# Row norms and final sums of the last projection listed behind the bank copy, three pairs of row tiles, another product order in the last pair, first-weight sums listed later, staging loads issued by GpSimd

## The chip, the core and the metric

The kernel runs on one core of a Trainium2 chip. The metric is the device time of one execution in microseconds (us), the median of several executions. All arithmetic is float32 or float32 split into two rounded parts.

## What is computed

One encoder layer is applied to two sequences of 1024 rows by 1024 channels (called 0 and 1 here). Cut to what matters:

```python
xn = rmsnorm(x, g_pre)
fv, fg, hv, hg, mg = split(xn @ w_in)
y_f = (real(fft2(fv)) * silu(fg)) @ w_fourier_out
v, x1, x2 = split(short_conv(hv))
z = v
for n, gate in enumerate((x1, x2)):
    z = gate * long_conv(z, filter[n])
y_h = (z * silu(hg)) @ w_hyena_out
g_f, g_h = split(sigmoid(mg + b_merge))
out = (g_f * y_f + g_h * y_h) @ w_out
return x + rmsnorm(out, g_post)
```

The last two lines are where most of the change lies: the last projection with `w_out`, then for each row of 1024 numbers the mean of the squares, its inverse root, the product with `g_post` and the sum with `x`.

## The kernel before

Every float32 operand of TensorE is split into a rounded part h and a rest l, and a product is three matmuls, h·h, h·l and l·h (`mm3`, `times`). ScalarE rounds (a CAST to h), and VectorE or GpSimd subtracts (the l). In rows of the profile, `wh` and `wl` are these parts of a weight block, `bh` and `bl` those of a data block.

There are three stages.

- `phase_fourier` makes the Fourier branch.
- `phase_main` first makes the filters' spectra, with projections of sequence 0 in between (`spill_gate`, `inproj`). In this stretch GpSimd subtracts the `wl` of each half weight block (128 by 512), one in 5 to 10 us, and TensorE waits in order for each of them. It then runs `branches`: the short and the long convolutions, first of sequence 0, then of sequence 1. For sequence 0 the weight parts are made and kept in DRAM (`d_w`); for sequence 1 they are loaded again by SyncE's queue (L728). The same queue loads the filter spectra (`k<-d_k`, L799) and stores results. During sequence 1 the generator `staging` (L912 ff.) reads blocks of three operands of the coming stage from DRAM in 24 pieces of 128 by 1024 (tiles `draw`, in two rooms, one for each half), GpSimd folds each piece in place (four subtractions or additions of 128 by 256), and GpSimd's queue stores it to `d_t` (and, unfolded, `d_wo` for `w_out`). The loads were issued by SyncE (L926), and the scheduler places them behind the load of a filter spectrum. Queues and engines work in order, so a load that waits for its room holds up whatever SyncE has listed behind it.
- `phase_blocks` does the rest of the projections as 34 jobs. A job makes a 256 by 1024 result from a 256 by 1024 and a 1024 by 1024 operand with seven block products instead of eight. Each product is 12 matmuls of 128 columns of weights and 512 columns of data, so a job is 84 matmuls. The products accumulate in three banks of PSUM, PA, PB and PC.

In `phase_blocks` the order on each engine is written by hand: every step is put in a list with a time, `at(t, step)`, the list is sorted, and each engine runs its own steps in this order. A job starts every 7 units, T = 7i. Job i's seven products stand at T + 0 ("11"), 2 ("12"), 3 ("s2"), 4 ("s3"), 6 ("s1"), and, within job i+1's first half, 8 ("s4") and 12 ("22"). So the order on TensorE within a job is: 11, s4 of the job before, 12, s2, s3, 22 of the job before, s1. The step that this text calls the bank copy is `seed` (L1142): ScalarE copies PA, which holds product 11, into PB, and only then may product 12 add to PB. Product s4 of the job before is the cover for that copy. `keep` (L1150) copies PA twice more, to `us` (U) and `m` (V), and `result` combines the banks with these copies into the four quarters (j, n) of a job's result: j is one of two blocks of rows or channels, n a half of 512 columns.

The last eight jobs (26 to 33, kind "o") are the last projection. Each makes two blocks of 128 rows. For each quarter `row_half` has ScalarE square it and sum the squares (`sq`, L1364, into `ss`), and VectorE multiply it with `g_post` (`o<-o,gp` or `o<-pg,gp`). `finish` then does the rest of the row norm on VectorE: an addition, two scalings and three Newton steps of three operations (L1375, L241 to L252; the case of one row has ten operations, L244 to L247), and four operations of 128 by 512 that multiply a quarter with the inverse root and add `x` (L177, `o<-o,rs,xr`), each followed by a store to the output from SyncE. `finish` of job i stood at T + 14, which is time 0 of job i+2. It is listed there ahead of quarter (1,1) of job i+1 (`o<-pg,m`), of that quarter's square on ScalarE, and of the bank copy of job i+2, which stands behind the square. The rows' tiles `o` took turns in two pairs of rooms (`xh4` to `xh7`), and `x` was loaded into one pair (`xh0`, `xh1`; `fetch_row`).

The weights of a job are prepared in `weights`: two blocks cast as they are ("11", "12"), then four sums on VectorE (`sum1`, `sum2`), and the casts and rests of the sums (`s2`, `s13`, `s4`) and of block "22". For the first job all of this stood some 24 units ahead of time 0, so ahead of the first bank copy at time 1.

Of the kernel before, what the change touches and what calls it, by code (L numbers as in the profile page):

```python
# [9 lines left out]
F32 = mybir.dt.float32  # L10
# [6 lines left out]
P = 128  # L17
D = 1024
# [143 lines left out]
class K:  # L162
# [748 lines left out]
    def staging(self):  # L911

        nc, a = self.nc, self.a
        before = None
        for q, k, half in [(q, k, h) for q in (1, 2, 5) for k in range(4) for h in range(2)] + [(0, 0, 0)]:
            r = None
            if q:
                s = slice(256 * half, 256 * half + 256)
                if half:
                    r = self.stage2.tile([P, 4, 256], F32, tag="draw2", name="draw", bufs=1)  # L920
                else:
                    r = self.cp.tile([P, 4, 256], F32, tag="draw", name="draw", bufs=1)
                with self.tc.issue_after(self.spectrum.ins):
                    for i in range(2):
                        src = {1: self.d_g[0][0], 2: self.d_sh[0]}[q][k + 4 * i] if q < 5 else a["w_out"][(k + 4 * i) * P:(k + 4 * i + 1) * P]
                        nc.sync.dma_start(r[:, 2 * i:2 * i + 2], src.rearrange("p (n c) -> p n c", n=2)[:, :, s])  # L926
            if before:
                q_, k_, s_, r_ = before
                if q_ == 5:
                    nc.gpsimd.dma_start(self.d_wo[:, k_, :, s_], r_)  # L930
                self.fold("pool", [r_[:, j] for j in range(4)])
                nc.gpsimd.dma_start(self.d_t[q_][:, k_, :, s_], r_)
            before = q, k, s, r
            yield
# [68 lines left out]
    def phase_blocks(self):  # L1003
# [24 lines left out]
        with ExitStack() as es:  # L1028
# [24 lines left out]
            def weights(j, t11, t12, ts, ts2, ts13, ts4, t22):  # L1053

                def part(t, n, pool, tags, bufs, src):

                    def open_():
                        A[j, n] = [pool.tile([P, 4, P], F32R, tag=g, name=g, bufs=bufs) for g in tags]
                    at(t, open_)
                    halve(t, lambda: (f2(A[j, n][0]), f2(A[j, n][1]), src()))  # L1060
                part(t11, "11", wp, ("wh", "wl"), 2, lambda: raw[j][:, 0])
                part(t12, "12", wp, ("wh", "wl"), 2, lambda: raw[j][:, 1])

                def sum1():
# [194 lines left out]
            for k in range(4):  # L1259
                at(start + 1 + 3 * k, xraw, k)  # L1260
                at(start + 3 + 3 * k, xfold, k)
            weights(0, start + 14, start + 14.1, start + 14.6, start + 15.8, start + 16, start + 16.2, start + 16.4)
            at(start + 11, load_raw, 1)

            PLACES = (None, ("X0", "X1", "E", "G1", "G2", "G0", "X2"), ("X3", "G3", "X0", "X1", "E", "G1", "G2"),
# [11 lines left out]
            for i in range(N):  # L1277
                T = SLOTS * i
                if i == N - 8:
                    at(T - 0.5, self.open_rows, op, jobs, gw)  # L1280
                kind = jobs[i][0]
                last = i + 1 == N
                for n, t in ((0, 0), (1, 2), (2, 3), (3, 4), (4, 6)):
                    at(T + t, product, i, n)
                if not last:
                    at(T + 8, product, i, 5)
                    at(T + 12, product, i, 6)
                at(T + 1, seed, i)
                at(T + 4, keep, i, U)
# [4 lines left out]
                result(i, 0, 0, T + 3.05)  # L1294
                result(i, 1, 1, T + 7.3)
                if not last:
                    result(i, 0, 1, T + 9.05)
                    result(i, 1, 0, T + 13.05)
# [4 lines left out]
                    weights(i + 1, T + 3.2, T + 4.3, T + 4.9, T + 5.7, T + 7.4, T + 9.3, T + 13.2)  # L1303
                    q = operand[i + 1]
                    if q != operand[i]:
                        turn(i, q)
                else:
                    def end():
                        pd = PC[i, 1] = self.psum("mm", 4, "pg")
                        self.times(pd, A[i, "22"], B[5, 3], True)  # L1310
                    at(T + 7, end)
                    at(T + 7.6, lambda: self.tt("dve", U[i], PC[i], U[i], SUB))

                    def row1():
                        self.tt("dve", self.rows[i][2][1][:, 0:512], PC[i, 1], U[i], ADD)
# [17 lines left out]

    def open_rows(self, op, jobs, gw):
        nc, a = self.nc, self.a
        self.op, self.jobs = op, jobs
        self.rows = {}
        self.gp = []
        for n in range(2):
            self.gp.append(gw.tile([P, 512], F32, tag="f", name="gp", bufs=4))  # L1340
            nc.sync.dma_start(self.gp[n], a["g_post"][0][512 * n:512 * n + 512].partition_broadcast(P))

    def open_row(self, i):
        xp = self.xp
        _, u, t = self.jobs[i]
        b, half = u // 2, u % 2
        row = [512 * half + P * t[j] for j in range(2)]
        ss = self.op.tile([P, 2, 2], F32, tag="ss", name="ss", bufs=2)
        o = [xp.tile([P, D], F32, tag=f"xh{4 + 2 * (i % 2) + j}", name="o", bufs=1) for j in range(2)]
        self.rows[i] = [b, row, o, None, ss]  # L1350

    def fetch_row(self, i):
        b, row = self.rows[i][:2]
        x = self.rows[i][3] = [self.xp.tile([P, D], F32, tag=f"xh{j}", name="xr", bufs=1) for j in range(2)]
        for j in range(2):
            self.nc.sync.dma_start(x[j], self.a[f"x{b}"][row[j]:row[j] + P, :])

    def row_half(self, at, t, i, j, n, src, made):
        nc = self.nc
# [9 lines left out]
    def finish(self, i, *rows):  # L1369
        nc, a, op = self.nc, self.a, self.op  # L1370
        b, row, o, x, ss = self.rows[i]
# [3 lines left out]
        nc.vector.tensor_tensor(s1, ss[:, rows[0]:rows[-1] + 1, 0], ss[:, rows[0]:rows[-1] + 1, 1], op=ADD)  # L1375
        self.rstd(op, rs, s1, n)
        for q, j in enumerate(rows):
            for n in (1, 0):
                s = slice(512 * n, 512 * n + 512)
                self.stt("dve", o[j][:, s], o[j][:, s], rs[:, q:q + 1], x[j][:, s], MUL, ADD)  # L1380
                nc.sync.dma_start(a[f"y{b}"][row[j]:row[j] + P, s], o[j][:, s])


def _chan_order():
    o = []
# [72 lines left out]
```

## Time and profile before

| what | us |
|---|---|
| median of three executions (2452.84 to 2453.99) | 2453.25 |
| profiled execution | 2460.39 |
| its span, from the first to the last instruction | 2458.49 |
| TensorE busy within the span | 2370.1 |
| VectorE busy | 2037.7 |
| ScalarE busy | 1126.2 |
| GpSimd busy | 561.7 |

The profile is of one execution, in us from its first instruction. Its own time is 1.90 above its span and 7.14 above the median. PE is TensorE's matmuls and PEld its weight loads, DVE is VectorE, ACT ScalarE, POOL GpSimd and SP SyncE; a q behind a name means the engine's queue, where DMAs are issued. In a row of the timeline stand the start, the duration, the engine, the line, the operation with the tiles that it writes and reads, the shape, and in brackets the idle time before it and what ended that. A row with a count merges neighbours that are alike. The duration of a matmul (0.39) is longer than the distance to the next one, since matmuls overlap. The granted clock is the share of TensorE's full clock.

### The profile page before, as it was taken

What the parts mean: (1) busy time and instruction counts of PE and PEld (TensorE: products, weight loads), DVE (VectorE), ACT (ScalarE), POOL (GpSimd) and SP (SyncE); (2) the same over time, 40 slices, a digit from 0 to 9 for tenths busy, and PEclk for the clock granted to TensorE, in tenths of its full rate; (3) what the DMA queues carried; (4) which work ended last, traced back from release to release, by engine and by line L of the source; (5) the groups of instructions that cost most, each with busy time, mean ns of one, the idle gap of its engine ahead of it and who ended that gap; (6) DMA issues with size and microseconds to landing.
All of it is one profiled execution on the core that took longest, in us unless ns stands there. A gap on an engine that the chain in (4) does not pass through costs nothing. (4 is left out here: it accounts for less than half of the span.)

```text
span 2458.5 us, 37126 instructions
## 1 busy us (share of the span) xinstructions
PE 2370.1 (96%) x13006; PEld 2055.8 (84%) x13006; DVE 2037.7 (83%) x3816; ACT 1126.2 (46%) x2088; POOL 561.7 (23%) x520
## 2 busy tenths in 40 slices
PE   6999999999989999999999999999999999999997
PEld 6988888888878988888889888888788888888775
DVE  7686788888889999999899999986667687776876
ACT  5545666666654333334222223233334466665532
POOL 1341222212234333442032333412100000101000
PEclk9999999999999999999999999999999999999999
DMA  8535644454556455555465667643556679888544
GB/s 272 173 136 196 221 157 157 156 160 161 166 190 202 161 178 176 160 161 195 151 212 184 215 206 228 214 141 112 205 180 219 234 260 286 257 275 244 160 153 137
DMA packets 253762, 470.26 MB, mean 191 GB/s; under 512 B 24502, under 2 KB 100503, under 8 KB 253192
## 3 DMA queue, kind: packets, MB, share of 16 engines
q1 hardware_dynamic: 230828, 393.12, 49.3%
q0 software_dynamic: 22560, 74.77, 9.2%
q8 instruction: 102, 1.67, 0.3%
q14 instruction: 84, 0.69, 0.1%
q10 hardware_dynamic: 188, 0.02, 0.0%
HBM read 300.04 MB, written 167.77 MB: 190 GB/s over the span
## 5 line engine op out<-in xcount | busy, mean ns | idle before, releaser
L194 PE MATMUL pin<-xh,wh 128*128 128x512 f32 x1472 | 578.1, 394 | 9.8 <-DMA wh<-d_w 5.6
L194 PE MATMUL pin<-xh,wl 128*128 128x512 f32 x1472 | 576.8, 393 | 4.2 <-DMA wl<-d_w 3.2
L194 PE MATMUL pin<-xl,wh 128*128 128x512 f32 x1472 | 577.9, 393 | 0.0
L181 POOL TENSOR_TENSOR wl<-wr,wh 128x512 fp32r<-128x512 f32 x136 | 252.8, 1859 | 748.1 <-ACT wh L171 719.8
L194 PEld LDWEIGHTS pin<-xh,wh 128*128 128x128 f32 x1472 | 278.1, 189 | 61.7 <-DMA wh<-d_w 6.4
L194 PEld LDWEIGHTS pin<-xh,wl 128*128 128x128 f32 x1472 | 278.1, 189 | 56.4 <-DMA wl<-d_w 4.1
L194 PEld LDWEIGHTS pin<-xl,wh 128*128 128x128 f32 x1472 | 278.2, 189 | 50.9
L194 PE MATMUL pT<-cinv,yh 128*128 128x256 f32 x1024 | 192.2, 282 | 0.0
L194 PEld LDWEIGHTS pT<-cinv,yh 128*128 128x128 f32 x1024 | 164.6, 190 | 9.4 <-ACT yh L171 0.4
L181 POOL TENSOR_TENSOR draw<-draw 128x256 f32<-128x256 f32 x96 | 108.9, 1134 | 250.2 <-DMA draw<-d_g 143.5
L181 DVE TENSOR_TENSOR t<-pX,k 128x1024 f32<-128x1024 f32 x128 | 155.5, 1215 | 8.3 <-PE pX L194 7.3
L171 ACT CAST yh<-y 128x512 fp32r<-128x512 f32 x128 | 79.5, 621 | 177.9 <-DVE y L181 152.0
L194 PE MATMUL pX<-bh,cfwd 128*128 128x256 f32 x768 | 160.5, 287 | 0.0
L171 ACT CAST wh<-wr 128x512 fp32r<-128x512 f32 x136 | 83.8, 616 | 159.3 <-PE pin L194 110.2
L171 ACT CAST bh<-b 128x512 fp32r<-128x512 f32 x144 | 88.7, 619 | 131.3 <-DVE b L181 90.7
L194 PE MATMUL pT<-cinv,yl 128*128 128x256 f32 x512 | 144.9, 283 | 1.1 <-DVE yl L181 1.1
L194 PEld LDWEIGHTS pX<-bh,cfwd 128*128 128x128 f32 x768 | 125.7, 191 | 3.1
L181 DVE TENSOR_TENSOR bl<-b,bh 128x512 fp32r<-128x512 f32 x144 | 112.1, 780 | 13.2 <-ACT bh L171 13.2
L194 PE MATMUL pX<-bl,cfwd 128*128 128x256 f32 x384 | 109.3, 285 | 0.0
L181 DVE TENSOR_TENSOR yl<-y,yh 128x512 fp32r<-128x512 f32 x128 | 92.7, 725 | 10.7 <-ACT yh L171 10.6
L1231 POOL DMA_DIRECT2D d_m<-gt x32 | 27.5, 860 | 320.7 <-DVE gt L181 290.5
L194 PEld LDWEIGHTS pT<-cinv,yl 128*128 128x128 f32 x512 | 97.7, 191 | 3.5 <-DVE yl L181 1.6
(351 smaller groups left out, 5712.5 us busy)
## 6 DMA issues: line engine op xcount, KB each, us to landing
k<-d_k SPq DMA_DIRECT2D x128, 512.0 KB, 4.4
wr<-in_w_in SPq DMA_DIRECT2D x136, 256.0 KB, 3.2
d_g<-gt SPq DMA_DIRECT2D x92, 256.0 KB, 2.6
d_k<-kt SPq DMA_DIRECT2D x128, 128.0 KB, 2.2
d_k<-kt SPq DMA_DIRECT2D x64, 256.0 KB, 2.3
fz<-d_g SPq DMA_DIRECT2D x64, 256.0 KB, 5.3
d_w<-wh POOLq DMA_DIRECT2D x48, 256.0 KB, 4.0
d_w<-wl POOLq DMA_DIRECT2D x48, 256.0 KB, 4.8
```

What stands on the lines that cost most here:

```text
L171: self.rounded = nc.scalar.copy(h, src)
L181: return e.tensor_tensor(out, a, b, op=op)
L194: return self.nc.tensor.matmul(out, lhsT, rhs, start=start, stop=stop, skip_group_check=shared)
L1231: at(t + 0.3, lambda: nc.gpsimd.dma_start(d_m[:, c], box[0], accum_op=ADD))
```

## The change

There are five edits.

1. `staging`: the loads of the pieces are issued by GpSimd and no longer by SyncE.
2. The first job's sums and all that follows from them are listed at times 0.2 to 2.4, behind the first bank copy.
3. `finish` is split in two. `root` holds the small operations and stands at T + 15.3, which is 1.3 of job i+2. `finish` holds the four long operations and stores, at T + 17.7 (3.7 of job i+2). Both are now behind the bank copy of job i+2 at its time 1.
4. Since rows live longer, `o` takes turns in three pairs of rooms (`xh2` to `xh7`), and `x` of odd jobs goes to rooms of its own (one tile of `op`, two tiles `f`). Each half row of `x` is a load of its own, four per job where there were two, and they stand at T + 5.3 (before: T + 8.9, in the last job T + 3).
5. The last pair: product 22 of job 32 stands at T + 9 (before: T + 12), and the last job's products 12, s2 and s3 stand one unit later. So TensorE's order in the last job is 11, s4 of job 32, 22 of job 32, 12, s2, s3, s1, and the closing two as before. The quarter (1,0) and the norm of job 32 move forward with it, ahead of quarter (1,1) of job 33. In the last job the inverse root of block 0 now stands ahead of the sums of block 1.

```diff
@@ staging
-  nc.sync.dma_start(r[:, 2 * i:2 * i + 2], src.rearrange("p (n c) -> p n c", n=2)[:, :, s])
+  nc.gpsimd.dma_start(r[:, 2 * i:2 * i + 2], src.rearrange("p (n c) -> p n c", n=2)[:, :, s])
@@ phase_blocks
-  weights(0, start + 14, start + 14.1, start + 14.6, start + 15.8, start + 16, start + 16.2, start + 16.4)
+  weights(0, start + 14, start + 14.1, 0.2, 1.1, 1.3, 2.1, 2.4)
...
+  early = i == N - 2
-  for n, t in ((0, 0), (1, 2), (2, 3), (3, 4), (4, 6)):
+  for n, t in enumerate((0, 3, 4, 5, 6) if last else (0, 2, 3, 4, 6)):
...
-  at(T + 12, product, i, 6)
+  at(T + (9 if early else 12), product, i, 6)
...
-  at(T + (8.9 if not last else 3), self.fetch_row, i)
+  at(T + 5.3, self.fetch_row, i)
...
-  at(T + 14, self.finish, i, 0, 1)
+  rows = [0, 1]
+  at(T + (11.3 if early else 15.3), self.root, i, rows)
+  at(T + (12.6 if early else 17.7), self.finish, i, rows)
...
-  at(T + 8.9, self.finish, i, 1)
+  at(T + 8.5, self.root, i, [1])
...
-  at(T + 10, self.finish, i, 0)
+  at(T + 9.4, self.root, i, [0])
+  at(T + 9.5, self.finish, i, [1])
+  at(T + 10, self.finish, i, [0])
@@ open_row, fetch_row
-  o = [xp.tile([P, D], F32, tag=f"xh{4 + 2 * (i % 2) + j}", name="o", bufs=1) for j in range(2)]
+  o = [xp.tile([P, D], F32, tag=f"xh{2 + 2 * (i % 3) + j}", name="o", bufs=1) for j in range(2)]
...
-  x = self.rows[i][3] = [self.xp.tile([P, D], F32, tag=f"xh{j}", name="xr", bufs=1) for j in range(2)]
+  if i % 2:
+      f = self.op.tile([P, D], F32, tag="xr", name="xr", bufs=1)
+      x = [[f[:, 0:512], f[:, 512:1024]], [self.gw.tile([P, 512], F32, tag="f", name="xr", bufs=4) for _ in range(2)]]
+  else:
+      x = [self.xp.tile([P, D], F32, tag=f"xh{j}", name="xr", bufs=1) for j in range(2)]
+      x = [[t[:, 0:512], t[:, 512:1024]] for t in x]
```

What this does to the order of instructions is seen at three places. The first is VectorE in a job in the middle of the last projection. Before, from the end of the norm of job i-2 on (the last Newton step, `rs`) to the rests `wl` of the next weights:

```order
L252 SCALAR_TENSOR_TENSOR rs<-rs_t,rs 128x2
L177 SCALAR_TENSOR_TENSOR o<-o,rs,xr 128x512 x4
L181 TENSOR_TENSOR o<-pg,m 128x512
L181 TENSOR_TENSOR o<-o,gp 128x512
L181 TENSOR_TENSOR s13l<-wraw,s13h 128x1024
L181 TENSOR_TENSOR o<-pg,gp 128x512
L181 TENSOR_TENSOR s4l<-wraw,s4h 128x512
L181 TENSOR_TENSOR o<-pg,gp 128x512
L181 TENSOR_TENSOR wl<-wraw,wh 128x512 x2
```

After, the same stretch (the eleven operations of `root` between L1387 and `o<-pg,gp` are left out):

```order
L181 TENSOR_TENSOR o<-pg,m 128x512
L181 TENSOR_TENSOR o<-o,gp 128x512
L181 TENSOR_TENSOR s13l<-wraw,s13h 128x1024
L1387 TENSOR_TENSOR s_25130<-ss 128x2
...
L181 TENSOR_TENSOR o<-pg,gp 128x512
L181 TENSOR_TENSOR s4l<-wraw,s4h 128x512
L181 TENSOR_TENSOR o<-pg,gp 128x512
L181 TENSOR_TENSOR wl<-wraw,wh 128x512
L177 SCALAR_TENSOR_TENSOR o<-o,rs,xr 128x512 x4
L181 TENSOR_TENSOR wl<-wraw,wh 128x512
```

The quarter `o<-pg,m`, for whose square the bank copy stands in line, has no norm ahead of it any more; the twelve small and the four long operations come later in the same job.

The second place is ScalarE at the first job. Before, the casts of the sums stand ahead of the bank copy (`pg<-pg`):

```order
L1034 CAST wh<-wraw 128x512
L768 COPY gt<-pin_19513 128x512
L1034 CAST s2h<-wsum 128x512
L1034 CAST s13h<-wraw 128x1024
L1034 CAST s4h<-wraw 128x512
L1034 CAST a2h<-wraw 128x512
L1142 COPY pg<-pg 128x512
```

After:

```order
L1034 CAST wh<-wraw 128x512
L768 COPY gt<-pin_19513 128x512
L1142 COPY pg<-pg 128x512
L1034 CAST s2h<-wsum 128x512
L1034 CAST s13h<-wraw 128x1024
L1034 CAST s4h<-wraw 128x512
L1034 CAST a2h<-wraw 128x512
```

Four casts have gone from ahead of the copy to behind it.

The third place is GpSimd in the stretch of the filters' spectra, far ahead of where the pieces were folded before. Before, from the load of the inverse tables (`cinv`) on, there stand only subtractions of weight rests, up to the first store of a kept weight block:

```order
L899 DMA cinv<-in_c_inv 128x6144
L181 TENSOR_TENSOR wl<-wr,wh 128x512 x53
L735 DMA d_w_0_0_189<-wh 128x512
```

After, from the twenty-eighth of them on (`d_g_0_4` and `d_g_0_1`, `d_g_0_5` are results that the same stretch stores to DRAM):

```order
L181 TENSOR_TENSOR wl<-wr,wh 128x512 x28
L926 DMA draw<-d_g_0_4_129 128x2x256 x2
L181 TENSOR_TENSOR wl<-wr,wh 128x512
L181 TENSOR_TENSOR draw<-draw 128x256 x8
L932 DMA d_t_241<-draw 128x4x256
L181 TENSOR_TENSOR wl<-wr,wh 128x512
L932 DMA d_t_241<-draw 128x4x256
L926 DMA draw<-d_g_0_1_126 128x2x256 x2
L181 TENSOR_TENSOR wl<-wr,wh 128x512 x6
L926 DMA draw<-d_g_0_5_130 128x2x256 x2
L181 TENSOR_TENSOR wl<-wr,wh 128x512
L181 TENSOR_TENSOR draw<-draw 128x256 x8
```

The folds of the first operand, two pieces at a time, now stand between subtractions that TensorE waits for; there are four such pairs in this stretch and at the start of `branches`. Those of the second operand follow as its blocks are stored, the first pair in the last part of sequence 0 and the others in sequence 1. On SyncE the 48 loads are gone. The order of the convolutions of sequence 1 on TensorE, VectorE and ScalarE, which the scheduler sets, differs in places as well.

More of the change, by code (lines that the diff above doesn't have):

```diff
@@ L1286, in phase_blocks @@
                     at(T + 8, product, i, 5)
-                    at(T + 12, product, i, 6)
+                    at(T + (9 if early else 12), product, i, 6)
                 at(T + 1, seed, i)
-                at(T + 4, keep, i, U)
+                at(T + (5 if last else 4), keep, i, U)
                 at(T + 7, keep, i, V)
@@ L1292, in phase_blocks @@
                     at(T + 2.9, self.open_row, i)
-                    at(T + (8.9 if not last else 3), self.fetch_row, i)
-                result(i, 0, 0, T + 3.05)
+                    at(T + 5.3, self.fetch_row, i)
+                result(i, 0, 0, T + (4.05 if last else 3.05))
                 result(i, 1, 1, T + 7.3)
@@ L1297, in phase_blocks @@
                     result(i, 0, 1, T + 9.05)
-                    result(i, 1, 0, T + 13.05)
+                    result(i, 1, 0, T + (10.05 if early else 13.05))
                     if kind == "o":
-                        at(T + 14, self.finish, i, 0, 1)
+                        rows = [0, 1]
+                        at(T + (11.3 if early else 15.3), self.root, i, rows)
+                        at(T + (12.6 if early else 17.7), self.finish, i, rows)
                     if i + 2 < N:
                         at(T + 6.7, load_raw, i + 2)
-                    weights(i + 1, T + 3.2, T + 4.3, T + 4.9, T + 5.7, T + 7.4, T + 9.3, T + 13.2)
+                    weights(i + 1, T + 3.2, T + 4.3, T + 4.9, T + 5.7, T + 7.4, T + 9.3, T + (10.3 if early else 13.2))
                     q = operand[i + 1]
@@ L1335, in open_rows @@
         nc, a = self.nc, self.a
-        self.op, self.jobs = op, jobs
+        self.op, self.jobs, self.gw = op, jobs, gw
         self.rows = {}
@@ L1348, in open_row @@
         ss = self.op.tile([P, 2, 2], F32, tag="ss", name="ss", bufs=2)
-        o = [xp.tile([P, D], F32, tag=f"xh{4 + 2 * (i % 2) + j}", name="o", bufs=1) for j in range(2)]
-        self.rows[i] = [b, row, o, None, ss]
+        o = [xp.tile([P, D], F32, tag=f"xh{2 + 2 * (i % 3) + j}", name="o", bufs=1) for j in range(2)]
+        self.rows[i] = [b, row, o, None, ss, {}]
     def fetch_row(self, i):
         b, row = self.rows[i][:2]
-        x = self.rows[i][3] = [self.xp.tile([P, D], F32, tag=f"xh{j}", name="xr", bufs=1) for j in range(2)]
+        if i % 2:
[4 more added lines that the diff above has]
+            x = [[t[:, 0:512], t[:, 512:1024]] for t in x]
+        self.rows[i][3] = x
         for j in range(2):
-            self.nc.sync.dma_start(x[j], self.a[f"x{b}"][row[j]:row[j] + P, :])
+            for n in range(2):
+                self.nc.sync.dma_start(x[j][n], self.a[f"x{b}"][row[j]:row[j] + P, 512 * n:512 * n + 512])
     def row_half(self, at, t, i, j, n, src, made):
@@ L1367, in row_half, with root @@
         at(t + d + 0.05, lambda: self.mul("dve", self.rows[i][2][j][:, s], src(), self.gp[n]))
-    def finish(self, i, *rows):
-        nc, a, op = self.nc, self.a, self.op
-        b, row, o, x, ss = self.rows[i]
+    def root(self, i, rows):
+        nc, op = self.nc, self.op
+        ss, rs_ = self.rows[i][4:6]
         n = len(rows)
@@ L1377, in finish @@
         for q, j in enumerate(rows):
+            rs_[j] = rs[:, q:q + 1]
+    def finish(self, i, rows):
+        nc, a = self.nc, self.a
+        b, row, o, x, _, rs = self.rows[i]
+        for j in rows:
             for n in (1, 0):
                 s = slice(512 * n, 512 * n + 512)
-                self.stt("dve", o[j][:, s], o[j][:, s], rs[:, q:q + 1], x[j][:, s], MUL, ADD)
+                self.stt("dve", o[j][:, s], o[j][:, s], rs[j], x[j][n], MUL, ADD)
                 nc.sync.dma_start(a[f"y{b}"][row[j]:row[j] + P, s], o[j][:, s])
```

## The prediction

> **What bounds the kernel now.** I read the page first, then the waits of TensorE over the whole span.
>
> ```profile
> span 2458.5 us, 37126 instructions
> PE 2370.1 (96%) x13006; PEld 2055.8 (84%) x13006; DVE 2037.7 (83%) x3816; ACT 1126.2 (46%) x2088; POOL 561.7 (23%) x520
> ...
> PE pg L194 <- ACT pg L1142: 14.3, 9, 2.9
> ...
> PE pin L194 <- DMA wh<-d_w: 5.6, 3, 4.5
> ...
> PE pin L194 <- DMA wl<-d_w: 3.2, 2, 3.1
> ```
>
> TensorE bounds the kernel: it stands idle for 88 us of 2458.5. No edit takes matmuls away, so every gain must come from this idle time, or from a slow clock behind it. A row of the waits gives the sum, the number of waits and the longest. The largest that the change touches is that for the bank copy: 14.3 us in 9 waits. Those for weights loaded by SyncE are 8.8 us in 5.
>
> A matmul costs (1777.43 - 1774.71) / 12 = 0.2267 us by these starts, so a product of 12 takes 2.72 and a job of 84 takes 19.04.
>
> ```profile
> 1774.71 0.39 PE L194 MATMUL pg<-xh,wh 128*128 128x512 f32 x1
> ...
> 1777.43 0.39 PE L194 MATMUL pg<-xh,wh 128*128 128x512 f32 x1
> ...
> 1780.66 0.79 PE L194 MATMUL pg<-xh,wh 128*128 128x512 f32 x1 [2.85 <-ACT pg L1142]
> ```
>
> **Part 1, the norm behind the bank copy.** The chain of waits names product 12 of jobs 27 and 33; the timeline shows what stands ahead of the second.
>
> ```profile
> 2298.66 11.19 PE pg L194 x48
> ...
> 2424.48 11.19 PE pg L194 x48
> ```
>
> ```profile
> 2417.49 0.15 DVE L1375 TENSOR_TENSOR s<-ss 128x2 f32<-128x2 f32 x1
> ...
> 2419.85 2.74 DVE L177 SCALAR_TENSOR_TENSOR o<-o,rs,xr 128x512 f32<-128x512 f32 x4
> 2422.51 0.68 DVE L181 TENSOR_TENSOR o<-pg,m 128x512 f32<-128x512 f32 x1
> ```
>
> ```profile
> 2417.46 0.59 ACT L1150 COPY m<-pg 128x512 f32<-128x512 f32 x1 [1.21 <-PE pg L194]
> 2423.22 0.63 ACT L1364 ACTIVATE sq<-o 128x512 f32<-128x512 f32 x1 [4.23 <-DVE o L181]
> ...
> 2423.85 0.58 ACT L1142 COPY pg<-pg 128x512 f32<-128x512 f32 x1
> ```
>
> `m` is ready at 2418.05, but `o<-pg,m` starts at 2422.51, because VectorE has begun the norm at 2417.49. The square and the bank copy follow, and product 12 starts at 2424.48, when the copy ends. From 2298.66 to there are six jobs: 125.82 us where six times 19.04 are 114.2. The excess is 11.6.
>
> With the norm behind it, `o<-pg,m` can start when `m` is there. Counted from the start S of product 11: `m` S + 0.6, the quarter S + 1.3, its square S + 1.9; product 11 ends at S + 2.9, the copy at S + 3.5. Product s4 covers TensorE until S + 5.44, so the copy has 1.9 us to spare and the stall goes whole. What is late next is VectorE's other work.
>
> ```profile
> 2403.53:2424.48 20.95, 19.33 (x84) 15.68 (x84) 15.29 (x33) 8.13 (x18) 0.00 (x0) 1.00 0.37 119
> ```
>
> In this row of the table of windows (length; then busy time of PE, PEld, DVE, ACT, POOL; granted clock), VectorE is busy for 15.29 of 20.95, and would be for 15.29 of 19.04. A hand-made schedule leaves about 1.3 us at the tightest wait. I take **-11.6**, with -5.8 as the poor end (half the stalls return) and nothing beyond.
>
> The three pairs of rooms and the separate `x` rooms only keep rows longer. The `x` loads (four issues where there were two) stand behind the stores and ahead of the next raw weights on SyncE, which then waits for a room; SyncE has the time of a job for some twelve issues, so I cost them at nothing. If that cover were gone, the raw weights would come late.
>
> **Part 2, the end.**
>
> ```profile
> 2440.81 2.74 DVE L177 SCALAR_TENSOR_TENSOR o<-o,rs,xr 128x512 f32<-128x512 f32 x4
> 2443.46 0.68 DVE L181 TENSOR_TENSOR o<-pg,m 128x512 f32<-128x512 f32 x1
> 2447.69 0.15 DVE L1375 TENSOR_TENSOR s<-ss 128x1 f32<-128x1 f32 x1
> 2449.79 1.42 DVE L177 SCALAR_TENSOR_TENSOR o<-o,rs,xr 128x512 f32<-128x512 f32 x2
> ...
> 2453.81 1.42 DVE L177 SCALAR_TENSOR_TENSOR o<-o,rs,xr 128x512 f32<-128x512 f32 x2
> ```
>
> ```profile
> 2443.47 0.39 PE L194 MATMUL pg<-bh,s4l 128*128 128x512 f32 x1
> ```
>
> The last matmul ends at 2443.86, VectorE's last operation at 2455.23: 11.4 us, then 3.26 for the last store. The last quarters wait for the norm of job 32, which the change moves ahead of them, together with product 22. Afterwards: the row of block 1 is ready 4.4 us after s1's end (the last combination, its square, and 2.1 for the root, 2449.79 - 2447.69), which is 1.7 after the last matmul; then quarter (0,1) 0.6, root 2.1, four long operations 2.75: 7.1 us instead of 11.4. **-4.3**; ends -2.7 (the 1.7 does not overlap as I think) and -4.3.
>
> **Part 3, the first weights.**
>
> ```profile
> 1777.44 0.62 ACT L1034 CAST s2h<-wsum 128x512 fp32r<-128x512 f32 x1 [1.60 <-DVE wsum L181]
> ...
> 1780.04 0.58 ACT L1142 COPY pg<-pg 128x512 f32<-128x512 f32 x1
> ```
>
> ```profile
> 1800.93 0.50 PE L194 MATMUL pg<-xh,wh 128*128 128x512 f32 x1 [0.66 <-ACT pg L1142]
> ```
>
> ```profile
> 1779.83:1786.65 6.82, 5.99 (x14) 4.73 (x15) 1.73 (x3) 1.25 (x3) 0.00 (x0) 0.50 0.00 0
> ```
>
> The first copy is ready to run when product 11 ends, but four casts are ahead of it, so TensorE waits 2.85 us. With them behind it the wait is that of 1800.93, where the copy is free to go: 0.66. That is 2.2. Behind the wait the granted clock is 0.50 for 6.82 us: 14 matmuls take 5.99 us where 14 times 0.2267 is 3.2, so 2.8 more. The first use of the moved sums, product s2, comes two products later than the copy; `s2h` and its rest need some 1.3 us behind the copy, which product 12 covers. I take **-5.0**, from -2.2 (the slow clock stays) to -5.0.
>
> The Trainium skill's page "TensorE: Matmul & The Clock Gate", Part 1, says that the clock goes to half after an idle window of about 3.4 us, free-running. By the length alone a wait of 2.85 would not cost clock, and this part would be worth 2.2 and the sum 23; the row shows 0.50 behind it, and the row decides.
>
> **Part 4, SyncE without the piece loads.**
>
> ```profile
> 1532.63 0.32 SPq L799 DMA_DIRECT2D k<-d_k  x1
> 1538.45 1.21 SPq L926 DMA_DIRECT2D draw<-in_w_out  x2
> 1539.75 0.54 SPq L728 DMA_DIRECT2D wh<-d_w  x1
> ```
>
> ```profile
> 1545.35 0.79 PE L194 MATMUL pin<-xh,wh 128*128 128x512 f32 x1 [4.55 <-DMA wh<-d_w]
> ...
> 1281.84 0.79 PE L194 MATMUL pin<-xh,wl 128*128 128x512 f32 x1 [3.10 <-DMA wl<-d_w]
> ```
>
> ```profile
> 1544.31:1551.13 6.82, 5.78 (x14) 4.52 (x15) 2.83 (x7) 0.00 (x0) 2.67 (x4) 0.50 0.59 213
> 1278.50:1286.00 7.50, 4.40 (x14) 3.34 (x13) 7.20 (x10) 0.14 (x1) 4.79 (x4) 0.77 0.71 272
> ```
>
> From 1532.95 to 1538.45 SyncE's queue stands at a piece load that waits for its room, and `wh` behind it is issued 5.5 us late; TensorE waits 4.55 for it. At 1281.84 it waits 3.10 for a `wl`, with piece loads ahead in the queue and DMA busy at 0.71. Behind them the slow clock costs 5.78 - 3.17 = 2.6 and 4.40 - 3.17 = 1.2. All this is 11.5. The first wait should go; the second may be the traffic's own, and the new place of the second operand's loads bunches traffic in the same stretch. I take **-8**, with ends -2 and -11.5.
>
> **Part 5, the pieces on GpSimd.** The loads take GpSimd's time, and those of the first operand now stand with their folds among the `wl` subtractions of sequence 0, with all behind them held.
>
> ```profile
> L181 POOL TENSOR_TENSOR draw<-draw x96: 724/826/4137, 1223.8 to 1587.0; 128x256 f32<-128x256 f32 x96
> L932 POOL DMA_DIRECT2D d_t<-draw x24: 772/772/797, 1234.4 to 1588.4; - x24
> ...
> DMA to landing us min/median/max: 3.2/5.1/8.0
> ```
>
> ```profile
> 542.61 0.32 SPq L774 DMA_DIRECT2D d_g<-gt  x1
> ```
>
> ```profile
> 556.22 1.30 POOL L181 TENSOR_TENSOR wl<-wr,wh 128x512 fp32r<-128x512 f32 x1 [9.46 <-PE pXf L194]
> ```
>
> ```profile
> 561.34 0.40 PE L194 MATMUL pin<-xh,wl 128*128 128x512 f32 x1
> ```
>
> At the pair of block 5: the block's last store is issued at 542.61; with the pieces' landing 5.1 as an estimate for it too, two issues 1.2, landing 5.1, eight folds, two stores 1.5 and the `wl` 1.3, that `wl` is ready 14.2 plus the folds later. TensorE needs it at 561.34, 18.7 later. The idle 9.46 ahead of it is what takes the folds in. At the median, 8 times 0.826 is 6.6, so it is 2.1 late; where the store lands as fast as the fastest piece (3.2), 0.2. There are four such pairs and one more of the second operand: between 0 and 5 times 2.1 is 10.5. I take **+3**, since two of the pairs have about one more us of room by my reading, and one comes after the stretch.
>
> The sum is -11.6 - 4.3 - 5.0 - 8 + 3 = -25.9. The span 2458.5 would be 2432.6. The profiled execution's own time, 2460.39, is 1.90 above its span and 7.14 above the median; the difference is applied to the median: 2453.25 - 25.9 = **2427.3**.
>
> **The rivals.**
>
> Half the stalls stay: VectorE becomes the bound of a job. For: the 1.3 us of slack is of a hand-made schedule. Against: 3.7 us of idle VectorE per job remain by 15.29 of 19.04. It gives 5.8 less, 2433.
>
> The copy was not waiting for the norm but for something as late. For: the wait is inferred. Against: `m` is ready 4.46 us ahead of `o<-pg,m`, and between 2417.49 and 2422.51 VectorE does nothing but the norm. It gives 11.6 less, 2439.
>
> Piece loads bunch: with GpSimd issuing them as rooms come free, new waits for `wh` or `wl` of `d_w` take the place of the old. For: DMA at 0.71 behind one of them. Part 4 is lost, and two waits of the old size come, 11.5 more: 2427.3 + 8 + 11.5 = 2447.
>
> Slower: GpSimd's queue, in order, holds `wl` back at all five places. If folds or issues there stretch as the longest of the row does (4.137 where the median is 0.826), one such fold per place makes it 2.1 + 3.3 = 5.4 late, and the slow clock behind a wait adds 2.8: 8.2 times 5 is 41, in place of 3: 2465. It decides the sign, slower by over 0.2% (4.9 us), from (25.9 + 3 + 4.9) / 5 = 6.8 us a place on. Against: the median fold is short, and 24 stores issued by GpSimd took 772 to 797 ns each in the crowded stretch, so issuing does not stretch there. The Trainium skill's page "SBUF — State Buffer", section "SBUF: two separate sides", says that a DMA issued by GpSimd has to write descriptors through the port pair that VectorE can lock, and that a DMA from SyncE's queue would not suffer; that speaks against this change. The issue rows of this trace do not bear it out, the longest fold may.
>
> **How the numbers follow.** Forecast 0.62, half the stalls 0.13, not the norm 0.05, bunching 0.12, held `wl` 0.04, anything else 0.04. The range 2418 to 2442 holds the first three, 0.80: its low end is all gains at their best without loss (11.6 + 4.3 + 5.0 + 11.5 = 32.4, 2421) less some 3 us for waits that I have not priced; its high end is 3 above the second rival. A change within 0.2%, 4.9 us, is about what a measurement of this kernel cannot tell from none. Faster by over that: forecast, first two rivals, and most of bunching, 0.89; same 0.06 (the rest of bunching and of what else may be), slower 0.05.
>
> **What would show it.** Right: in the profile after, product 12 of jobs 28 to 33 follows without a wait for the copy, and jobs are 19.0 to 19.2 us apart; last matmul to VectorE's last end is 7 us; the granted clock stays at 1.00 behind the first copy, whose wait is below 1; no wait of 4.5 near 1540. Wrong: idle time of TensorE ended by VectorE or the copy in the last jobs; a wait for `wl` from GpSimd between 480 and 720; new waits for `d_w` between 1250 and 1450.

## The result and the profile after

The changed kernel takes 2438.86 us (median of 6 runs, 2438.35 to 2440.13), the kernel before 2454.55 beside it (2452.84 to 2460.11): a ratio of 0.9934, with a 95% interval of 0.9922 to 0.9947. That is 15.7 us faster where 25.9 were forecast. The spans of the two profiled executions differ by 21.3, 2458.49 and 2437.2, because the one before, at 2460.39, was slower than all six of these.

The page, and the same rows of TensorE's waits as before (sum, number, longest):

```profile
span 2437.2 us, 37123 instructions
PE 2366.3 (97%) x13006; PEld 2053.1 (84%) x13006; DVE 2034.0 (83%) x3816; ACT 1126.2 (46%) x2088; POOL 563.5 (23%) x568
...
PE pXf L194 <- DVE kt L177: 6.4, 7, 2.1
...
PE pg L194 <- ACT pg L1142: 3.0, 3, 1.7
...
PE pXf L194 <- DVE bl L181: 2.2, 2, 1.2
PE pin L194 <- POOL wl L181: 2.1, 2, 1.3
PE pin L194 <- DMA wh<-d_w: 1.9, 2, 1.5
```

The wait for the bank copy is down from 14.3 to 3.0, the waits for `d_w` from 8.8 to 1.9. The three other rows have grown: `pXf` waits for VectorE's `kt` and `bl`, and `pin` for GpSimd's `wl`. Before they were:

```profile
PE pXf L194 <- DVE kt L177: 2.5, 5, 0.6
...
PE pXf L194 <- DVE bl L181: 1.2, 1, 1.2
...
PE pin L194 <- POOL wl L181: 0.9, 1, 0.9
```

All these waits lie ahead of 740, in the stretch of the filters' spectra and at the start of `branches`, but for one for `wl` at 1133.

**The jobs.** The chain names one run of matmuls from product 12 of job 27 to the last product but one, and the row of windows (length; busy PE, PEld, DVE, ACT, POOL; clock) shows a job's time without a gap:

```profile
2293.49 130.89 PE pg L194 x576
```

```profile
2404.50:2423.55 19.05, 19.05 (x86) 15.78 (x85) 16.02 (x42) 5.80 (x14) 0.00 (x0) 1.00 0.43 153
```

VectorE's and ScalarE's rows show why. The quarter starts as soon as `m` is there, the copy waits for product 11 alone, and the norm's four long operations come eight us after the copy:

```profile
2403.26 0.69 DVE L181 TENSOR_TENSOR o<-pg,m 128x512 f32<-128x512 f32 x1 [0.31 <-ACT m L1150]
...
2413.55 2.73 DVE L177 SCALAR_TENSOR_TENSOR o<-o,rs,xr 128x512 f32<-128x512 f32 x4
```

```profile
2405.36 0.57 ACT L1142 COPY pg<-pg 128x512 f32<-128x512 f32 x1 [0.57 <-PE pg L194]
```

**The end.** The last matmul ends at 2427.09, VectorE at 2433.84: 6.75 us, where 11.4 stood before and 7.1 were forecast.

```profile
2426.70 0.39 PE L194 MATMUL pg<-bh,s4l 128*128 128x512 f32 x1
```

```profile
2431.11 2.73 DVE L177 SCALAR_TENSOR_TENSOR o<-o,rs,xr 128x512 f32<-128x512 f32 x4
```

**The first weights.** The copy is listed ahead of the casts and the wait is the 0.66 that was read off job 1:

```profile
1778.82 0.50 PE L194 MATMUL pg<-xh,wh 128*128 128x512 f32 x1 [0.66 <-ACT pg L1142]
```

**Where time was lost.** I compared the start of each matmul with that of the same matmul in a second trace of the kernel before (e4 below, span 2449.9), by the median over stretches of 80 us. Positive is later:

| stretch (us) | changed kernel | edits 2 to 5 alone (e2) |
|---|---|---|
| 320 to 400 | +0.8 | -1.4 |
| 720 to 800 | +11.6 | +2.5 |
| 1040 to 1120 | +11.6 | +2.5 |
| 1200 to 1280 | +15.5 | +1.8 |
| 1600 to 1680 | +6.1 | -1.6 |
| 1840 to 1920 | +3.9 | -3.8 |
| span | -12.7 | -18.4 |

The changed kernel loses 10.9 between 400 and 720 and 3.9 near 1130, gains 9.4 between 1200 and 1600, 2.2 at the first weights and 16.6 in the jobs and at the end. The order of e2 is that of before up to the first weights, so its +3.9 and -3.4 on the way there are the spread of two executions: one trace tells such sums to some 4 us.

The scheduler's order is not what costs between 400 and 720. In the changed kernel VectorE's order there is that of before, TensorE's differs at one place near 508, and ScalarE's and SyncE's in a few places behind 620. In e9 below TensorE has the order of before, and the loss is there all the same.

### The profile page after: what moved, and what is told of

The parts are those of the page before. It is cut to its first block, busy times and chain, and to the rows that moved or that the text cites. A ratio compares the mean times of both kernels' runs of the same rounds, so it can differ in the third digit from the quotient of the medians.

```text
span 2437.2 us, 37123 instructions
## 1 busy us (share of the span) xinstructions
PE 2366.3 (97%) x13006; PEld 2053.1 (84%) x13006; DVE 2034.0 (83%) x3816; ACT 1126.2 (46%) x2088; POOL 563.5 (23%) x568
## 4 chain that ended last, share of the span: by engine, by line
PE 50%; DMA 1%; DVE 1%; issue 0%; ACT 0%; SPq 0%; DVEq 0%; ACTq 0%
PE pg L194 25%; PE pin L194 16%; PE pT L194 4%; PE pX L194 4%; DMA wh<-d_w 1%; PE tph L787 1%; DMA bl<-d_t 0%; DMA wraw<-d_m 0%; DVE bl L181 0%; DVE wraw L181 0%; DVE gt L181 0%; DVE o L181 0%; DVE o L177 0%; ACT bh L1034 0%; ACT pg L1142 0%
## 5 line engine op out<-in xcount | busy, mean ns | idle before, releaser
L181 POOL TENSOR_TENSOR wl<-wr,wh 128x512 fp32r<-128x512 f32 x136 | 243.5, 1790 | 885.0 <-ACT wh L171 657.4
L181 DVE TENSOR_TENSOR y<-t 128x512 f32<-128x512 f32 x128 | 97.6, 763 | 0.8
```

The costliest lines, as they stand in the source:

```text
L181: return e.tensor_tensor(out, a, b, op=op)
```

## The experiments

Ratios are to runs of the kernel before on the same chip, with 95% intervals. Theory A: edit 1 loses more in sequence 0 than it gives back in sequence 1, and edits 2 to 5 carry the whole gain. The rival B is the prediction's own sum.

**e1, edit 1 alone**

```diff
 (before)
-  nc.sync.dma_start(r[:, 2 * i:2 * i + 2], src...)
+  nc.gpsimd.dma_start(r[:, 2 * i:2 * i + 2], src...)
```

> The kernel before with edit 1 alone (the piece loads issued by GpSimd). Theory A, from the two traces: the folds among the weight subtractions of sequence 0 cost 11.4 us between 440 and 735, of which the relieved queue of SyncE gives back 2 to 8 in sequence 1, so 3 to 9 us slower than before. Rival B, the prediction's terms: -8 + 3, so 5 us faster. In the trace A wants a loss of some 11 us against before between 440 and 735, with TensorE's waits ended by VectorE (kt, bl, acc) and not by GpSimd's wl.

2460.69 against 2453.47, ratio 1.0029 (1.0019 to 1.004): 7.2 slower. A stands, B falls. Its trace loses 11.4 between 400 and 720, with waits for the tiles that the changed kernel waits for there (`kt`, `bl`, `wh`).

**e2 and e12, edits 2 to 5 without edit 1**

```diff
 (changed kernel)
-  nc.gpsimd.dma_start(r[:, 2 * i:2 * i + 2], src...)
+  nc.sync.dma_start(r[:, 2 * i:2 * i + 2], src...)
```

> The changed kernel with the piece loads issued by SyncE again (edits 2 to 5 alone). Theory A: -11.6 - 4.3 - 5.0 = 20.9 us faster than before, so 2433 to 2434, some 5 us faster than the changed kernel; sequence 0 runs as before. Rival B: without edit 1 its gain of 5 goes, so the changed kernel's 2438.9 becomes 2444. A third theory, that something in edits 2 to 5 gave less than the trace shows, would have it at 2439 or above with sequence 0 as before.

> Edits 2 to 5 again, beside e11 on the same chip: 2434 within the spread of its five runs (2430 to 2438).

2434.09, ratio 0.992 (0.9909 to 0.9932), and the second time 2433.40, ratio 0.9915 (0.9895 to 0.9936). This is 19 to 21 us faster than before and some 5 faster than the changed kernel, which bears out A again.

**e3, GpSimd issues the loads, but no earlier than before**

`issue_after` orders only instructions of the engine of its anchor, a load on SyncE. With the pieces on GpSimd it bound nothing; that is why they moved into sequence 0. Here the order is put back by an edge of its own, without a wait.

```diff
-  with self.tc.issue_after(self.spectrum.ins):
+  ld = nc.gpsimd.dma_start(...)
+  self.tc.add_manual_dep(ld.ins, self.spectrum.ins.name, <order only>)
```

> The changed kernel with GpSimd issuing the piece loads, but listed no earlier than before (each pair behind the same spectrum load in the order, as the loads on SyncE were), so that no fold stands in sequence 0. Theory A: the loss of 11.4 in sequence 0 goes and the relief of SyncE in sequence 1 stays: 2428 to 2434, as fast as or faster than edits 2 to 5 alone. A theory in which GpSimd issuing the loads is what costs (not the place of the folds) has it at 2438 or above, with loads or folds that take longer than 0.8 us in sequence 1.

2433.26, ratio 0.9916 (0.9904 to 0.9928). Taken alone, the intervals of e2, e12 and e3 overlap that of the changed kernel; that all three lie some 5 us below it is what tells them apart. In the trace of e3 the loss in sequence 0 is gone, so the pieces' place is what costs, and not who issues them. But it is no faster than e2. The relief of SyncE, -8 in the prediction, is not to be seen in the total.

**e4, the kernel before once more**

> The kernel before, unchanged: a second trace of it. If the waits for wh and wl at 1278 and 1540 (7.98 us of stalls and 3.8 of slow clock) belong to every execution, they stand here with the same lengths and the span is near 2458. If they belong to the slower of its executions (2452.84 to 2460.11 measured), one of them is missing or shorter and the span is near 2451.

2451.78. The wait of 4.55 for `wh` near 1540 is not there. Another has taken its place, for a `wl` that GpSimd has ready late (POOL's queue, then TensorE):

```profile
1542.34 7.58 POOL L181 TENSOR_TENSOR draw<-draw 128x256 f32<-128x256 f32 x4 [6.14 <-DMA d_wo<-draw]
1550.22 0.77 POOL L932 DMA_DIRECT2D d_t<-draw  x1 [0.30 <-POOL draw L181]
1551.01 1.27 POOL L181 TENSOR_TENSOR wl<-wr,wh 128x512 fp32r<-128x512 f32 x1
```

```profile
1552.34 0.80 PE L194 MATMUL pin<-xh,wl 128*128 128x512 f32 x1 [3.43 <-POOL wl L181]
```

And behind the first bank copy, where TensorE waits 2.85 (3.01 by its starts) as in the first trace, the granted clock is 1.00 and not 0.50:

```profile
1774.92:1780.92 6.00, 5.99 (x26) 4.98 (x27) 2.19 (x4) 1.31 (x3) 0.00 (x0) 1.00 0.13 45
```

So which wait stands near 1540, and whether the clock falls behind a wait of 3 us, differs between executions of one kernel.

**e5 and e6, the first operand without folds and with twice the folds**

```diff
-  self.fold("pool", ...)
+  if q_ != 1: self.fold("pool", ...)                        (e5)
+  for _ in range(2 if q_ == 1 else 1): self.fold("pool", ...)   (e6)
```

> The changed kernel without the 64 folds of the first operand; its pieces are still loaded and stored by GpSimd among the weight subtractions of sequence 0 (the arithmetic of that operand is left out). Theory A1, it is GpSimd's folds that cost there: the loss between 400 and 735 goes, so 2431 to 2434. Rival A2, it is the pieces' traffic and the loads and stores that wait in GpSimd's queue: the loss stays, 2437 to 2439.

> The changed kernel with the folds of the first operand done twice (so its values are others). A1: 6.5 us more of GpSimd at each of four places in sequence 0, of which the idle time there no longer takes any: 10 us or more on top of the changed kernel, 2449 and above. A2: 2439 to 2442.

e5 takes 2446.83, ratio 0.997 (0.9959 to 0.9981), and e6 2440.93, ratio 0.9944 (0.9932 to 0.9956). Both contradict A1: without folds it is slower, and twice the folds cost 2 us, which the intervals do not tell from none. e6 lies where A2 wants it, e5 outside of both. e5 says less than it was meant to: without the folds the scheduler lists the work of sequence 0 in another order, TensorE's from about 500 on and VectorE's from about 535, and a wait of 5.7 for VectorE that begins near 724 stands in that order, so its time is not the folds' alone. e6 keeps VectorE's order of the changed kernel, and between 400 and 660 it loses some 6 us against e2 where the changed kernel loses 8.6. GpSimd's time as such is not the cost.

**e7, the norm at its old place, all else of edits 2 to 5 kept**

```diff
-  at(T + (11.3 if early else 15.3), self.root, i, rows)
-  at(T + (12.6 if early else 17.7), self.finish, i, rows)
+  at(T + (11.3 if early else 14), self.root, i, rows)
+  at(T + (12.6 if early else 14), self.finish, i, rows)
```

> Edits 2 to 5 (piece loads by SyncE) with the root and the four long operations of the norm both listed at the old time, ahead of quarter (1,1), but with the three pairs of rooms, the new loads of x and the reordered last pair kept. If the norm ahead of the quarter is what delayed the bank copy, the waits of 1.6 to 1.8 stand again before product 12 of jobs 28 to 32, perhaps not 33, where product 22 adds cover: 5 to 6 times 1.78, so 8.9 to 10.7 more than edits 2 to 5: 2443 to 2445. If the rooms or the loads made the difference: 2434.

2444.32, ratio 0.9959 (0.9946 to 0.9972), 10.2 more than e2. VectorE and TensorE in the job that follows:

```profile
2387.13 2.74 DVE L177 SCALAR_TENSOR_TENSOR o<-o,rs,xr 128x512 f32<-128x512 f32 x4
2389.79 0.68 DVE L181 TENSOR_TENSOR o<-pg,m 128x512 f32<-128x512 f32 x1
```

```profile
2391.76 0.73 PE L194 MATMUL pg<-b,wh 128*128 128x512 f32 x2 [1.62 <-ACT pg L1142]
```

Before, the same wait was:

```profile
2403.53 0.73 PE L194 MATMUL pg<-b,wh 128*128 128x512 f32 x2 [1.62 <-ACT pg L1142]
```

The wait of 1.62 is back, to the hundredth. The rooms and the loads of `x` did not bring the gain; they only allow it.

**e8, edits 3 to 5 alone**

```diff
 (e2)
-  weights(0, start + 14, start + 14.1, 0.2, 1.1, 1.3, 2.1, 2.4)
+  weights(0, start + 14, start + 14.1, start + 14.6, start + 15.8, start + 16, start + 16.2, start + 16.4)
```

> Edits 3 to 5 alone (piece loads by SyncE, first sums at their old time). Against edits 2 to 5 (2434.1) the wait before the first product 12 is 2.2 longer. If the slow clock behind it (2.8) is there in every execution, 5.0 more: 2439.1; if it is there in none or few, 2.2 to 3 more: 2436.3 to 2437.

2438.3, ratio 0.9932 (0.9916 to 0.9947): 16.0 faster than before, with an interval of 13 to 21. Edit 2 is the 4.2 between it and e2, but six runs spread from 2430.9 to 2443.5, so this does not tell 2.2 from 5.0. The traces do in part: of four with the long first wait, the clock behind it is 0.50 in one (the first of before), 0.74 over 6 us in one (e1), 1.00 in two (e4, e8).

**e9, thin loads**

```diff
+  if q == 1 and k and not i: nc.gpsimd.memset(r, 1.0)
+  c_ = slice(0, 2) if q == 1 and k else slice(0, 256)
-  nc.gpsimd.dma_start(r[:, 2 * i:2 * i + 2], src...[:, :, s])
+  nc.gpsimd.dma_start(r[:, 2 * i:2 * i + 2, c_], src...[:, :, s][:, :, c_])
```

> The changed kernel with the loads of the first operand's pieces cut to 2 of 256 columns for three of the four pairs (GpSimd fills the room by a memset instead, and the values are others); the folds and the stores stay where they are. The loss of the changed kernel between 400 and 735 against edits 2 to 5 is 7 to 8.6 us in the trace. Theory C, it has two parts: VectorE's operations that stand beside a fold, and waits of kt for its store while the pieces are loaded; C wants the kt waits ended by the d_k store (5.9 us in all) to go and the stretched VectorE operations to stay, a loss of 3 to 6. If the traffic of the loads is all, the loss goes (below 2). If the folds are all, it stays at 7 or above.

2445.74, ratio 0.9972 (0.996 to 0.9983). VectorE's waits of `kt` for its store are gone, as C wanted. But the loss against e2 between 400 and 735 grew to some 12 instead of shrinking, which C did not expect. It lies where the expectation would have it if the folds were all; that it grew was in none of the theories. VectorE and GpSimd at the second pair show why:

```profile
544.48 8.00 DVE L181 TENSOR_TENSOR bl<-b,bh 128x512 fp32r<-128x512 f32 x1
552.40 0.41 DVE L181 TENSOR_TENSOR T<-pft,ex 128x256 f32<-128x256 f32 x1
552.74 0.68 DVE L181 TENSOR_TENSOR bl<-b,bh 128x512 fp32r<-128x512 f32 x1
```

```profile
543.74 1.44 POOL L929 DMA_DIRECT2D draw<-d_g  x2 [6.84 <-DMA d_g<-gt]
545.20 1.29 POOL L181 TENSOR_TENSOR wl<-wr,wh 128x512 fp32r<-128x512 f32 x1
546.45 5.48 POOL L181 TENSOR_TENSOR draw<-draw 128x256 f32<-128x256 f32 x8
```

A subtraction that takes 0.68 a little later takes 8.00: it starts beside the second of two load issues, 0.7 ahead of a `wl`, lies over this `wl` and eight folds that GpSimd runs without a gap, and ends 0.6 after them. In the changed kernel the folds wait 0.36 and 0.44 for their loads. TensorE waits 6.4 for the subtraction.

**e10, only the loads of `w_out` on GpSimd, and e11, all of them behind sequence 0**

```diff
+  ld = (nc.gpsimd if q == 5 else nc.sync).dma_start(...)   (e10, with the order edge of e3)
-  with self.tc.issue_after(self.spectrum.ins):
+  with self.tc.issue_after(self.gated.ins):                (e11; gated: GpSimd's last product x2 of sequence 0)
```

> Edits 2 to 5, with GpSimd issuing only the loads of the third operand's pieces (w_out), listed no earlier than before; the others are issued by SyncE. The held wh of d_w near 1535 (2.64 and the slow clock behind it in the trace of edits 2 to 5) goes if the w_out load that waits for its room is what holds SyncE's queue: 2429 to 2432 against 2434.1. If another wait takes its place, as in the kernel with all loads on GpSimd: 2433 to 2435.

> The changed kernel with GpSimd issuing all piece loads, listed behind GpSimd's last product of sequence 0 (the gate x2) and otherwise as early as they can be. Theory D: no fold stands beside VectorE's work between 400 and 735, so that loss (7 to 9) goes; all pieces are done well ahead of the wl near 1550, so the wait for wh or wl there goes too, as in the changed kernel; new waits of some 3 to 6 us in all where pieces and d_w weights share the DMA engines between 1130 and 1400. 2428 to 2434, at or below edits 2 to 5. If sequence 1 has no place for the folds of the first operand either, it is 2436 or more.

e10 takes 2443.3, ratio 0.9956 (0.994 to 0.9973): worse than e2 by 9, and outside of both expectations. In its trace, of an execution of 2447.14 where six lie between 2438.8 and 2449.05, the wait for `wh` is gone, and one of 15.59 for GpSimd's `wl` has come:

```profile
1558.82 0.76 POOL L931 DMA_DIRECT2D d_wo<-draw  x1 [4.87 <-DMA draw<-in_w_out]
1562.24 3.12 POOL L181 TENSOR_TENSOR draw<-draw 128x256 f32<-128x256 f32 x4 [2.67 <-DMA d_wo<-draw]
1565.65 0.77 POOL L933 DMA_DIRECT2D d_t<-draw  x1 [0.30 <-POOL draw L181]
1566.45 1.27 POOL L181 TENSOR_TENSOR wl<-wr,wh 128x512 fp32r<-128x512 f32 x1
```

```profile
1567.78 0.80 PE L194 MATMUL pin<-xh,wl 128*128 128x512 f32 x1 [15.59 <-POOL wl L181]
```

The `wl` stands behind two pieces in GpSimd's queue, each with a wait for a load and for a store. The order of TensorE also differs from e2's in places from 1524 on, so not all of the 15.59 need be the queue's.

e11 gives 2439.97, ratio 0.9938 (0.9918 to 0.9959): its trace, of an execution of 2444.69 where six lie between 2431.77 and 2444.69, loses nothing in sequence 0 and some 18 us against e12 between 1120 and 1400, in many small delays and in waits for `d_w`, `yh` and `t`. Theory D fell: bunched in sequence 1 the pieces cost 6.6 against e12 by the medians, about what they cost in sequence 0, though these two intervals overlap.

## Why the prediction was right or wrong

**Part 1 and 2: right, in mechanism and size.** -11.6 and -4.3 were forecast, 15.9 together; e8 measured 16.0 for these edits, and e7 shows the norm's place as the cause of the larger part. That the two agree to 0.1 is chance: the interval of e8 is 13 to 21, and after 1840 the traces give these edits 12.7 (e8) to 16.6 (the changed kernel). VectorE was not the next bound: the row of 19.05 has it busy for 16.02. The two rivals on this part (half the stalls stay; the copy waited for something else) fall.

**Part 3: the wait right, its price too sure.** The wait shrank to 0.66 as said. The 2.8 for the slow clock were taken from the only trace at hand, as if every execution had it, with -2.2 as the poor end. Two of four traces have none of it. The Trainium skill's page "TensorE: Matmul & The Clock Gate", Part 1, calls the window free-running, and these traces agree: one and the same wait of 2.85 is followed by 0.50, 0.74 and twice by 1.00. The page has the clock fall after an idle window of about 3.4 us; here it fell in two of four traces at 2.85, and the measurement decides. The prediction quoted the page for the window's length and let the row decide; it should have taken the word free-running as the reason that one row cannot.

**Part 4: the term that was mis-sized, -8.** It was read from one trace, of an execution of 2460.39. Its wait of 4.55 for `wh` is 2.5 to 3.0 in three traces with SyncE's queue as before (e2, e7, e12) and missing in two (e4, e8); in e4 a `wl` holds its place. The changed kernel does gain 9.4 against e4 between 1200 and 1600, since its pieces are all done by 1375 (they ended at 1588 before) and that `wl` is on time, but it loses 3.9 just ahead of that. The same matmuls, from 1040 to 1680 in e4, take:

| kernel | us |
|---|---|
| before, two traces (first, e4) | 642.4, 639.9 |
| edit 1 alone (e1) | 639.9 |
| SyncE's queue as before, some or all of edits 2 to 5 (e2, e7, e8, e12) | 635.8, 636.2, 633.8, 634.8 |
| the queue relieved, pieces paced (e3) | 635.8 |
| changed kernel | 634.3 |

The six traces of the first and third rows have one and the same order of instructions up to 1680, and they differ among themselves by more than relieving the queue changes, alone (e1) or with the other edits (e3, the changed kernel). In place of -8 the runs show nothing beyond the spread of executions.

**Part 5: the step that failed, +3.** It priced GpSimd being late with `wl`, and that hardly happened: all waits for `wl` add up to 2.1 us. What it left out is what GpSimd's work does to VectorE. In the changed kernel, at the pair that the prediction worked out:

```profile
545.54 1.44 POOL L926 DMA_DIRECT2D draw<-d_g  x2 [6.84 <-DMA d_g<-gt]
547.00 1.29 POOL L181 TENSOR_TENSOR wl<-wr,wh 128x512 fp32r<-128x512 f32 x1
548.65 0.80 POOL L181 TENSOR_TENSOR draw<-draw 128x256 f32<-128x256 f32 x1 [0.36 <-DMA draw<-d_g]
```

```profile
546.27 2.58 DVE L181 TENSOR_TENSOR bl<-b,bh 128x512 fp32r<-128x512 f32 x1
```

```profile
548.91 0.39 PE L194 MATMUL pXf<-bl,cfwd 128*128 128x256 f32 x1 [1.00 <-DVE bl L181]
...
558.84 0.36 PE L194 MATMUL pXf<-bh,cfwd 128*128 128x256 f32 x1 [2.09 <-DVE kt L177]
```

The load of `d_g` waits in GpSimd's queue for its block's store, so the `wl` behind it comes 1.4 later in VectorE's work than in e2, and falls upon the whole of `bl`: 2.58 where e2 has 1.45. TensorE waits at once. In e2:

```profile
541.73 1.52 POOL L181 TENSOR_TENSOR wl<-wr,wh 128x512 fp32r<-128x512 f32 x1 [6.35 <-ACT wh L171]
```

```profile
542.35 1.45 DVE L181 TENSOR_TENSOR bl<-b,bh 128x512 fp32r<-128x512 f32 x1
```

The second cost is VectorE's wait for room to write `kt`, which the store of an earlier `kt` frees. The group row of the changed kernel from 430 to 735 (busy, mean | idle before, and what ended it), and that of e2:

```profile
L177 DVE SCALAR_TENSOR_TENSOR kt<-pXf,th,ktmp 128x128 f32<-128x128 f32 (+1 forms) x130 | 41.9, 373 | 15.7 <-DMA d_k<-kt 5.9 <-ACT ktmp L672 3.8 <-DMA sg<-d_g 3.2
```

```profile
L177 DVE SCALAR_TENSOR_TENSOR kt<-pXf,th,ktmp 128x128 f32<-128x128 f32 (+1 forms) x135 | 43.2, 374 | 10.8 <-ACT ktmp L672 3.8 <-DMA wr<-in_w_in 3.2 <-ACT ktmp L682 2.6
```

The 5.9 is new: no trace without pieces in this stretch has it. e9, with thin loads, has none of it, but e6, which moves the same bytes as the changed kernel, has none either, so the traffic alone does not make it; what does stays open.

The first cost can be summed. The 645 operations that VectorE runs in e4 between 400 and 735 stand in the same order in these traces (waits are those over 0.15 us):

| trace | busy with them | waits | from the first to the last |
|---|---|---|---|
| no pieces there (the two of before, e2, e3, e7, e8, e10, e11, e12) | 279.7 to 280.7 | 53.0 to 56.4 | 333.4 to 337.1 |
| changed kernel | 285.6 | 57.5 | 343.3 |
| edit 1 alone (e1) | 286.3 | 56.0 | 342.2 |
| twice the folds (e6) | 301.3 | 41.0 | 342.3 |
| thin loads (e9) | 297.7 | 52.3 | 350.2 |

With the pieces beside it VectorE needs 5 to 6 us more for the same work. Its waits do not shrink for it, so this is more than half of the 6 to 10 by which the stretch grows, and it is what the term of +3 left out. In e6 it needs 21 more but waits 13 less: much of what the second set of folds adds falls into time in which VectorE would have waited anyway. How the rest divides between the `kt` waits and the holding stays open, since every variant that takes one away moves the other.

**The rivals.** Neither "bunching" (0.12) nor "GpSimd holds `wl`" (0.04) came in the changed kernel but in small waits: 1.5 for a `wh` at 1291, 0.8 for a `wl` at 700 and 1.3 for one at 1133. Both mechanisms exist in another order: e11 shows the first, e10 the second at one place, for up to 15.59. In the changed kernel edit 1 costs 5 us with the other edits (e2 against it) and 7.2 alone, where the prediction had a gain of 5. That difference of 10 is the whole error: 25.9 forecast, 15.7 measured. That the measured time lies within the stated range all the same is luck in part: the high end, 2442, was set by the second rival, which did not come, and VectorE held by GpSimd was in no term.

## What to carry to other kernels

Work that moves to an idle engine is priced by what that engine shares with the critical one, and not only by whether it is in time. An order constraint tied to an instruction on one engine is lost when the work goes to another engine: look at where the order puts it. And a stall that hangs on a race of transfers, or a clock drop behind it, is worth its mean over several traces and not its row in one. Leaving edit 1 out (2433.4 to 2434.1) or pacing it (2433.3) beats the kernel before and, by some 5 us, the changed one.

## What the runs showed of the hardware

VectorE's `bl` took 8.00 us while GpSimd ran nine operations back to back, and 0.68 beside none (e9); it ended 0.6 after them, and the folds, 5.48 for eight, were not stretched. The Trainium skill's page "SBUF — State Buffer", section "SBUF: two separate sides", describes a port pair locked by one of the two for a whole instruction; the runs agree, and add that a chain of GpSimd operations can keep VectorE out from the first to the last. One thing does not fit: the page gives the pair to the one that starts first, and by the profile `bl` starts 0.7 ahead of the `wl`. The page also says there that an operation of VectorE in a two-port mode keeps GpSimd from writing the descriptors of its DMAs. Nothing of that kind shows: in the changed kernel's rows of the tiles `draw`, an issue took 704 to 753 ns, and a load landed at most 7.6 us after its issue began, where the longest of SyncE's took 8.0 before.

```profile
L926 POOL DMA_DIRECT2D draw<-d_g x16: 709/724/753, 253.5 to 673.0; - x16
L926 POOL DMA_DIRECT2D draw<-d_sh x16: 704/722/752, 867.2 to 1268.5; - x16
L926 POOL DMA_DIRECT2D draw<-in_w_out x16: 704/717/729, 1280.6 to 1360.5; - x16
```
